# Output tiles split behind the row statistics, an MLP bank read earlier, the first tile's plane in halves, and attention's sums with ones at the head of a step

## The chip, the cores and the metric

One core of one Trainium2 chip. The time is device time in microseconds of one execution of the whole kernel. TensorE (PE) multiplies matrices into PSUM banks, VectorE (DVE), ScalarE (ACT) and GpSimd (POOL) do the elementwise work, and SyncE (SP) issues most DMAs. Each engine takes its instructions strictly in the order of its own queue.

## The reference

A bidirectional encoder block on a sequence of 1024 rows, width 1024, in float32:

```python
h = layer_norm(x, ln0_g, ln0_b)
proj = h @ w_in + b_in                 # 4352 columns: qa ka va qb kb vb ga gb
y_na  = neighbourhood_attention(qa, ka, va, na_rpb) @ w_branch_na
y_swa = windowed_gqa_with_sink(rope(qb), rope(kb), vb, sink) @ w_branch_swa
mixed = sigmoid(ga) * y_na + sigmoid(gb) * y_swa
h = layer_norm(ALPHA * h + mixed @ w_out + b_out, ln1_g, ln1_b)
u = square(relu(h @ w_ff1 + b_ff1))    # 4096 wide
h = layer_norm(ALPHA * h + u @ w_ff2 + b_ff2, ln2_g, ln2_b)
```

## The kernel before

**Numbers.** A float32 matrix is held as two float16 planes: the high plane is the matrix times a scale, rounded (made by ACT), the low plane is what the rounding left (made by DVE). A product is three PE matmuls for each slice of 128: high with high, high with low, low with high. The scale of a matrix comes from the sum of its squares: ACT squares with an accumulator, a small PE matmul with a matrix of ones adds up the partitions into two columns of a bank, DVE reads them, POOL raises them to a power. That matmul is the "sum with ones" (`total_of`, L194; its reader is `scale_of`, L200).

**Order.** The program runs under a manual schedule: each engine executes in the order in which the Python code issues instructions to it. So a moved line moves its instructions in each engine's queue. Stages that follow each other:

- *First layer norm* (8 tiles of 128 rows). Statistics on DVE, power on POOL, the norm itself on ACT (L369) or on DVE (L367) for the tiles listed in `NO_DVE` (index 2 and 3, which are tiles 6 and 7). PE turns each 128x128 block (L386), `ln0_turn` makes the planes `hT`, and gate projections run in between (L430).
- *Attention in 64 steps* (`steps`). A step issues scores for step s+2 (`part_a`: PE writes banks s and t, DVE reduces them, L783), then fill matmuls of the projections (`pump`), the exponentials and the low planes (`part_e`, `part_l`, whose planes are turned by DMA), more fill, the product with v (`part_c`), and the last fill. Jobs put off with `defer(n, ...)` become due after n fill matmuls and are issued by `flush`. Entry 2 of such a job says that it begins with PE work: sums with ones for the weights (L194), which write into spare columns of the newest score bank, and the turn of the softmax's reciprocals (L839). Both are issued by the `flush()` behind `part_c`.
- *Branch products* (`branch(f, half)`, 8 chunks of 128 columns by 2 halves). Bank gi=0 is the neighbourhood branch, gi=1 the window branch; DVE scales each bank with its gate (L1540), POOL adds the two into `mx` (L1542), ACT squares `mx` (`mx_square`, L1485). In the second half `between` issues the next chunk's sum with ones inside bank gi=1; in the very last one it issues `mx_scale(0)`: DVE adds the eight sums (`mx_sum`, L1489), PE totals (L1495), DVE reads (L1497), POOL takes the power (L1498), and `split_mx(0)` makes the planes of tile 0 (L1509 ACT, L1510 DVE).
- *Output products* for g = 0 to 7 (tiles of 128 rows), each in two banks of 512 columns (`out_mm`, L1637 to L1644). `out_evac` adds the residual and takes statistics (DVE, L1651 and L1655), `ln1_norm` finishes them (DVE L1659 and L1660, POOL L1661 and L283, ACT L285). The turn of tile g-1 (`turn`, L1672) stands in the middle of the second bank of tile g, its evacuation (`turn_evac`, ACT L1683 and DVE L1680) behind it, then `combine(g-1)` makes operand planes for the MLP (L1688, L1689; sums L1702 to L1706 from tile 4 on). `split_mx(g+2)` comes right behind the first bank's matmuls. `bound` (in g = 0) reads a bank of a small sum (DVE, L320) and computes a scale on POOL (L321 to L328), which `turn_evac(0)` uses. `late` (POOL, L1825) scales residual rows of later tiles. In g = 5 the first two weight slices of the MLP are split (`head_split`, L1736 ACT, L1739 DVE).
- *First MLP product* (16 column blocks p; `ff1_mm(p, i)`, L1812). Each block takes seven half-size products (a Strassen-Winograd scheme), i in the order 1, 2, 6, 5, 7, 3, 4, with weight sums (L1777) and operand sums S1 to S4. `after1(p, 1)` copies a bank (ACT, L1911) and settles the block before (ACT L1934, L1935 and a store), `after1(p, 2)` reads bank "s" (DVE, L1931). Bank "s" has two buffers. The first products run in the order (0,1) (0,2) (1,1) (1,2), turn of tile 7, (2,1) (2,2) (3,1) (3,2), (0,6) (1,6) (0,5) (1,5); `tick` prepares their weights, `comb_hi` and `comb_lo` their operands.
- *Second MLP product* (L2278) and the last layer norm.

Of the kernel before, what the change touches and what calls it, by code (L numbers as in the profile page):

```python
# [22 lines left out]
NCG = 8  # L23
# [46 lines left out]
STATS = {2: (4,), 3: (5,), 4: (6,)}  # L70
NO_DVE = 2, 3
NO0=4
# [21 lines left out]
def encoder_block(ctx, tc, x, w_in, w_br, w_out, w_ff1, w_ff2, par, rows, rpbp,  # L94
# [345 lines left out]

    def flush(pe=True, early=False, mid=False):
        for e in list(later):
            if e[0] <= 0 and (pe or not e[2]) and (e[3] or not early) and (early or not e[4] or not in_steps) \
                    and (mid or not e[5] or not in_steps):
                later.remove(e)
                e[1][0]()
                if e[1][1:]:
                    defer(*e[1][1:], early=e[3])
# [491 lines left out]
    with tc.manual_schedule(engines=MANUAL):  # L940
# [110 lines left out]
        def steps(s, n, before_b=None, before_c=None):  # L1051

            part = [int(n * SPLIT[0]), int(n * SPLIT[1])]
            part.append(n - sum(part))
            step_now[0] = s
            if s + 2 < 64:
                part_a(s + 2)
            pump(part[0])
            if before_b:
                before_b()  # L1060
            for op in bias_ops[:3]:
                bias_ops.pop(0)()
            flush(False, True)
            if 0 <= s + 1 < 64:
                part_l(s + 1)
            part_e(s + 2)
            if 0 <= s + 2 < 64 and (s + 2) % 8 == 7:
                norm_rows(heads[(s + 2) // 4].get()[5])
            flush(False, mid=True)
            pump(part[1])  # L1070
            if before_c:
                before_c()
            if s >= C_LAG:
                part_c(s - C_LAG)
            flush()
            pump(part[2])
# [399 lines left out]
        def tok(g):  # L1476
            return slice(g * P, (g + 1) * P)
# [14 lines left out]
        def mx_scale(half, ps, ones_, pw_):  # L1492
            if half == 0:
                mx_sum(0)
            PE.matmul(ps[:, 0:2], ones_, mtot[:, half:half + 1].to_broadcast([P, 2]), start=True, stop=True)  # L1495
# [7 lines left out]
        def split_mx(g):  # L1503

            if g < 2:
                xm.append(xps[g].tile([P, 2, 2, 8, P], F16, tag="m", name="m"))
            m = xm[g % 2][:, g // 2 % 2]
            mhl[g] = m[:, 0], m[:, 1]
            ACT.activation(m[:, 0], mx[:, :, tok(g)], AF.Copy, bias=0.0, scale=mx_sc(g, 0))  # L1509
            DVE.scalar_tensor_tensor(out=m[:, 1], in0=mx[:, :, tok(g)], scalar=mx_sc(g, 0), in1=m[:, 0],  # L1510
                                     op0=ALU.mult, op1=ALU.subtract)

# [14 lines left out]
        def branch(f, half, between=None):  # L1527
            both = []
            for gi, (act, tag) in enumerate(((o_na, "t"), (o_swa, "o"))):
                ps = psum(tag)  # L1530
                n = 2 if gi and between else 4
                gemm3(ps, bws[f], lambda part, k: act(part, k, half), nk=n, k0=4 * gi, last=(n == 4))
                if n == 2:
                    between()
                    gemm3(ps, bws[f], lambda part, k: act(part, k + 2, half), nk=2, k0=6, first=False)
                if (f, half, gi) == (7, 1, 1):
# [292 lines left out]
    with tc.manual_schedule(engines=MANUAL):  # L1829
# [10 lines left out]
        for g in range(NCG):  # L1840
            out_mm(g, 0, 0, 8)
            if g + 2 < NCG:
                split_mx(g + 2)
            if g + 2 < NCG:
                pre(g + 2)
# [25 lines left out]
            if 2 <= g < 6:  # L1871
                squares1(g - 2, raws[g - 2])
            if g == 5:
                head_split(0, 1)
                head_split(0, 2)
            out_evac(g, 1)
            ps = bound_sum() if g == 0 else None
            ln1_norm(g)
            if g == 0:
# [88 lines left out]
        ff1_mm(1, 2)  # L1968
        turn(7)
        turn_evac(7)  # L1970
        more_ring(1)
# [71 lines left out]
        tick()  # L2043
        after1(1, 1)
        after1(1, 2)
        tick()
# [525 lines left out]
```

## Time and profile before

| | |
|---|---|
| median of 3 runs | 1237.51 us (1237.05 to 1238.98) |
| the profiled execution's own time | 1237.68 us |
| its span, first to last instruction | 1235.7 us |
| granted PE clock | 0.998 |
| busy PE / DVE / ACT / POOL | 1210.1 / 976.1 / 867.3 / 333.9 us |
| attention's steps | about 85 to 388 us |
| branch products end, output products start | 548.8 us |
| output products end, first MLP product starts | 640.7 us |

A row of the timeline gives start, length (both us), engine, line, operation, output and inputs, shape and count; in brackets stands how long the engine had been idle and what ended that. Successive rows of an engine overlap by about 0.1 us, as an instruction's last part overlaps the start of the next. A row of the table of waits gives who waited for whom, the total, the number of times and the longest.

### The profile page before, as it was taken

How to read it: one execution, taken by the hardware profiler on the slowest of the kernel's cores; microseconds unless marked ns; L12 is line 12 of the kernel's file. 1: busy time of each engine (PE TensorE's matmuls, PEld its weight loads, DVE VectorE, ACT ScalarE, POOL GpSimd, SP SyncE). 2: the span in 40 equal slices, each digit the busy share in tenths (PEclk: the TensorE clock that was granted, in tenths of full speed). 3: DMA queues.
4: the chain of work that ended last, by engine and by line, in shares of the span. 5: the costliest groups of instructions: out<-in, count | busy, mean ns of one | idle time of the engine just before them, and what ended most of it. 6: DMA issues, size and time to landing. Idle time of an engine off the chain costs nothing.

```text
span 1235.7 us, 17241 instructions
## 1 busy us (share of the span) xinstructions
PE 1210.1 (98%) x6070; PEld 606.1 (49%) x6070; DVE 976.1 (79%) x1421; ACT 867.3 (70%) x1418; POOL 333.9 (27%) x368
## 2 busy tenths in 40 slices
PE   7999999999999999999999999999999999999997
PEld 5545555555555444444544444444444444444443
DVE  7687998878887975655798887887867778897888
ACT  7569889998886569743758878778775846344457
POOL 5212222433520013437620031333200002211207
PEclk9999999999999999999999999999999999999999
DMA  8654758777675346526513466776536536363333
GB/s 314 202 186 107 161 147 173 178 164 168 144 161 159 109 154 230 188 78 245 193 63 119 166 212 218 265 242 235 197 136 235 223 132 231 124 261 128 124 111 136
DMA packets 177878, 216.84 MB, mean 175 GB/s; under 512 B 111744, under 2 KB 125312, under 8 KB 171136
## 3 DMA queue, kind: packets, MB, share of 16 engines
q1 hardware_dynamic: 176816, 214.89, 54.7%
q8 instruction: 47, 0.77, 0.3%
q10 hardware_dynamic: 976, 0.87, 0.2%
q14 instruction: 39, 0.32, 0.1%
HBM read 130.69 MB, written 59.33 MB: 154 GB/s over the span
## 4 chain that ended last, share of the span: by engine, by line
PE 78%; DVE 8%; ACT 6%; issue 2%; POOL 2%; DMA 1%; SPq 0%; POOLq 0%; ACTq 0%; DVEq 0%
PE ps_mm L430 14%; PE ps_t L1812 6%; PE ps_o L1812 6%; PE ps_mm L1812 6%; PE ps_mm L2278 6%; PE ps_s L2278 6%; PE ps_t L2278 5%; PE ps_o L2278 5%; PE ps_s L1812 3%; PE ps_o L889 2%; PE ps_o L1178 2%; PE ps_mm L1178 1%; PE ps_t L1178 1%; PE ps_t L420 1%; PE ps_t L421 1%
## 5 line engine op out<-in xcount | busy, mean ns | idle before, releaser
L430 PE MATMUL ps_mm<-hT 128*128 128x512 f16 x960 | 226.4, 380 | 4.5 <-DVE hT L399 2.0
L1812 PEld LDWEIGHTS <-tw 128*128 128x128 f16 x1248 | 122.1, 99 | 145.0 <-DVE tw L1739 0.8
L2278 PEld LDWEIGHTS <-r1w 128*128 128x128 f16 x1008 | 98.7, 98 | 118.4
L430 PEld LDWEIGHTS <-hT 128*128 128x128 f16 x960 | 90.7, 99 | 102.0 <-issue 12.0
L802 ACT ACTIVATE ss<-ss,sk 128x384 f32<-128x384 f32 (+1 forms) x128 | 73.8, 578 | 25.3 <-DVE sk L783 25.1
L430 PE MATMUL ps_mm<-hT,wpair 128*128 128x512 f16 x288 | 68.8, 380 | 0.0
L1733 POOL TENSOR_TENSOR c<-c 128x2 f32<-128x2 f32 x16 | 15.6, 977 | 189.0 <-DVE c L1732 189.0
L2298 POOL TENSOR_TENSOR acc<-acc,rst 128x512 f32<-128x512 f32 x16 | 32.2, 2013 | 122.1 <-DMA rst<-xr_d 77.8
L201 POOL TENSOR_TENSOR hT<-hT 128x2 f32<-128x2 f32 x30 | 25.6, 852 | 114.1 <-DVE hT L200 114.1
L2112 ACT ACTIVATE hA<-r1w,c 128x2048 f16<-128x2048 f32 x10 | 20.0, 1996 | 50.0 <-DVE r1w L2167 26.8
L1739 DVE SCALAR_TENSOR_TENSOR tw<-raw,c,tw 128x512 f16<-128x512 f32 x60 | 51.2, 853 | 4.2 <-ACT tw L1736 3.9
L2115 DVE SCALAR_TENSOR_TENSOR r1w<-stg,c,r1w 128x2048 f16<-128x2048 f32 x21 | 49.6, 2360 | 4.0 <-ACT r1w L2112 4.0
L2278 PEld LDWEIGHTS <-hS 128*128 128x128 f16 x336 | 32.9, 98 | 39.4
L1178 PEld LDWEIGHTS <-hT 128*128 128x128 f16 x336 | 32.8, 99 | 38.6 <-DVE hT L1167 0.8
L889 PE MATMUL ps_o<-pt,vv 128*128 128x256 f16 (+1 forms) x448 | 49.2, 250 | 2.2 <-DMA pt<-hT 1.5
L814 DVE SCALAR_TENSOR_TENSOR pl<-ss,pl 128x768 f16<-128x768 f32 (+1 forms) x42 | 46.3, 1101 | 2.2 <-ACT pl L805 2.0
L1998 DVE TENSOR_TENSOR hS<-hS,hS 128x512 f32<-128x512 f32 x41 | 33.6, 820 | 14.6 <-ACT hS L1929 14.5
L889 PEld LDWEIGHTS <-vv 128*128 128x128 f16 x448 | 35.5, 98 | 19.3 <-DVE oT L898 1.9
L1812 PE MATMUL ps_t<-hS,tw 128*128 128x512 f16 x192 | 44.1, 379 | 0.3 <-DVE tw L1739 0.3
L1812 PE MATMUL ps_t<-r1w,tw 128*128 128x512 f16 x192 | 44.0, 379 | 0.0
L1812 PE MATMUL ps_o<-r1w,tw 128*128 128x512 f16 x192 | 44.0, 379 | 0.0
L1736 ACT ACTIVATE tw<-raw,c 128x512 f16<-128x512 f32 x60 | 41.8, 709 | 2.8 <-DVE raw L1777 2.8
(443 smaller groups left out, 3140.8 us busy)
## 6 DMA issues: line engine op xcount, KB each, us to landing
us_d<-hS SPq DMA_DIRECT2D x112, 256.0 KB, 3.1
stg<-us_d SPq DMA_DIRECT2D x28, 1024.0 KB, 4.8
raw<-in_w_ff SPq DMA_DIRECT2D x24, 512.0 KB, 5.6
r1w<-in_w_ff SPq DMA_DIRECT2D x10, 1024.0 KB, 7.6
sg<-sg_d SPq DMA_DIRECT2D x32, 256.0 KB, 2.9
hT<-in_w_in SPq DMA_DIRECT2D x60, 128.0 KB, 2.6
hA<-in_w_ff SPq DMA_DIRECT2D x6, 1024.0 KB, 8.2
hT<-in_w_in SPq DMA_DIRECT2D x11, 512.0 KB, 4.7
```

The lines of the kernel that those rows point to most:

```text
L430: PE.matmul(ps, a[:, k, :], act(b, k), start=(k == 0 and i == 0), stop=(k == NK - 1 and i == 2))
L802: ACT.activation(p, p, AF.Exp, bias=nm[:, i:i + 1], scale=-1.0, accum_out=sums_l[o_chunk][:, hh, 2 * t + i:2 * t + i + 1])
L814: DVE.scalar_tensor_tensor(out=pl[:, n:2 * n], in0=e[:, 0:n], scalar=P_SCALE, in1=pl[:, 0:n], op0=ALU.mult, op1=ALU.subtract)
L889: PE.matmul(o, vs, move(part), start=(m == 0 and part == 0), stop=(m == len(runs) - 1 and part == 1))
L1178: PE.matmul(ps, w[:, a, k, :], act[:, b, k, :], start=(first and k == 0 and m == 0), stop=(k == 3 and m == 2), skip_group_check=True)
L1736: ACT.activation(hi_lo(slot, 0), src, AF.Copy, bias=0.0, scale=w_scale(p))
L1739: DVE.scalar_tensor_tensor(out=hi_lo(slot, 1), in0=src, scalar=w_scale(p), in1=hi_lo(slot, 0), op0=ALU.mult, op1=ALU.subtract)
L1812: PE.matmul(ps, ww, act[:, part, k, :], start=(first and k == 0 and m == 0), stop=(k == 3 and m == 2), skip_group_check=True)
L1998: DVE.tensor_tensor(out=out, in0=a, in1=b, op=op)
L2115: DVE.scalar_tensor_tensor(out=slot[:, :, 1, :], in0=src, scalar=scale, in1=slot[:, :, 0, :], op0=ALU.mult, op1=ALU.subtract)
L2278: PE.matmul(ps, st[:, a, part, j * P:(j + 1) * P], w[:, a, wpart, :], start=(first and a == 0 and m == 0), stop=(a == 3 and m == 2), skip_ ...
L2298: POOL.tensor_tensor(out=z, in0=z, in1=t, op=ALU.add)
```

## The change

- The norms of tiles 6 and 7 of the first layer norm go to ACT (`NO_DVE` is empty).
- `flush` gets a `head` form, which issues only the jobs that begin with PE work; `steps` calls it first of all. The `flush` behind `part_c` no longer issues such jobs.
- In the branch products `between` is issued after one slice (three matmuls) of bank gi=1 and no longer after two. `mx_sum(0)` is issued ahead of the matmuls of bank gi=0 of the last chunk.
- `split_mx(0)` works in two halves of four slices each, on ACT and DVE in turn.
- In the output products `split_mx(g+2)` is issued behind `ln1_norm(g)`, and the two `head_split` of g = 5 as well. `bound` keeps its place in the text, and so comes behind the split of tile 2.
- `after1(1, 1)` and `after1(1, 2)` are issued right behind `turn(7)`, ahead of its evacuation.

```diff
--- before.py
+++ after.py
@@ -68,7 +68,7 @@
 PREP = 5, 6, 7, 8, 8, 9, 10, 12, 13, 14, 15, 16
 HI_ACT = (0, 2, 3, 4, 5), ()
 STATS = {2: (4,), 3: (5,), 4: (6,)}
-NO_DVE = 2, 3
+NO_DVE = ()
 NO0=4
 N_GATES = (2,), (3,), (4,), (), (5, 6, 7)
 SPLIT = .25, .45
@@ -438,9 +438,9 @@
 
         later.append([fns[0], fns[1:], pe, early or only, only, mid])
 
-    def flush(pe=True, early=False, mid=False):
+    def flush(pe=True, early=False, mid=False, head=False):
         for e in list(later):
-            if e[0] <= 0 and (pe or not e[2]) and (e[3] or not early) and (early or not e[4] or not in_steps) \
+            if e[0] <= 0 and (e[2] or not head) and (pe or not e[2]) and (e[3] or not early) and (early or not e[4] or not in_steps) \
                     and (mid or not e[5] or not in_steps):
                 later.remove(e)
                 e[1][0]()
@@ -1053,6 +1053,7 @@
             part = [int(n * SPLIT[0]), int(n * SPLIT[1])]
             part.append(n - sum(part))
             step_now[0] = s
+            flush(head=True)
             if s + 2 < 64:
                 part_a(s + 2)
             pump(part[0])
@@ -1072,7 +1073,7 @@
                 before_c()
             if s >= C_LAG:
                 part_c(s - C_LAG)
-            flush()
+            flush(False)
             pump(part[2])
 
         for n in range(0, N_PRE, 4):
@@ -1490,8 +1491,6 @@
                               op=ALU.add)
 
         def mx_scale(half, ps, ones_, pw_):
-            if half == 0:
-                mx_sum(0)
             PE.matmul(ps[:, 0:2], ones_, mtot[:, half:half + 1].to_broadcast([P, 2]), start=True, stop=True)
             t = mxc[:, 4:6]
             DVE.tensor_scalar(out=t, in0=ps[:, 0:2], scalar1=Q_MIN, scalar2=W_TOP ** -2, op0=ALU.max, op1=ALU.mult)
@@ -1506,9 +1505,10 @@
                 xm.append(xps[g].tile([P, 2, 2, 8, P], F16, tag="m", name="m"))
             m = xm[g % 2][:, g // 2 % 2]
             mhl[g] = m[:, 0], m[:, 1]
-            ACT.activation(m[:, 0], mx[:, :, tok(g)], AF.Copy, bias=0.0, scale=mx_sc(g, 0))
-            DVE.scalar_tensor_tensor(out=m[:, 1], in0=mx[:, :, tok(g)], scalar=mx_sc(g, 0), in1=m[:, 0],
-                                     op0=ALU.mult, op1=ALU.subtract)
+            for ks in (slice(0, 4), slice(4, 8)) if g == 0 else (slice(0, 8),):
+                ACT.activation(m[:, 0, ks], mx[:, ks, tok(g)], AF.Copy, bias=0.0, scale=mx_sc(g, 0))
+                DVE.scalar_tensor_tensor(out=m[:, 1, ks], in0=mx[:, ks, tok(g)], scalar=mx_sc(g, 0), in1=m[:, 0, ks],
+                                         op0=ALU.mult, op1=ALU.subtract)
 
         sg, sgs = {}, [(f, gi, half) for f in range(8) for half in range(2) for gi in range(2)]
 
@@ -1528,11 +1528,13 @@
             both = []
             for gi, (act, tag) in enumerate(((o_na, "t"), (o_swa, "o"))):
                 ps = psum(tag)
-                n = 2 if gi and between else 4
+                n = 1 if gi and between else 4
+                if (f, half, gi) == (7, 1, 0):
+                    mx_sum(0)
                 gemm3(ps, bws[f], lambda part, k: act(part, k, half), nk=n, k0=4 * gi, last=(n == 4))
-                if n == 2:
+                if n == 1:
                     between()
-                    gemm3(ps, bws[f], lambda part, k: act(part, k + 2, half), nk=2, k0=6, first=False)
+                    gemm3(ps, bws[f], lambda part, k: act(part, k + 1, half), nk=3, k0=5, first=False)
                 if (f, half, gi) == (7, 1, 1):
                     split_mx(0)
                 s_ = sg[f, gi, half]
@@ -1840,8 +1842,6 @@
         for g in range(NCG):
             out_mm(g, 0, 0, 8)
             if g + 2 < NCG:
-                split_mx(g + 2)
-            if g + 2 < NCG:
                 pre(g + 2)
             out_evac(g, 0)
             if g == 1:
@@ -1870,12 +1870,14 @@
                     head_hi(3, i, tsp.tile([P, 2, 512], F16, tag="ts", name="tws", bufs=4))
             if 2 <= g < 6:
                 squares1(g - 2, raws[g - 2])
+            out_evac(g, 1)
+            ps = bound_sum() if g == 0 else None
+            ln1_norm(g)
             if g == 5:
                 head_split(0, 1)
                 head_split(0, 2)
-            out_evac(g, 1)
-            ps = bound_sum() if g == 0 else None
-            ln1_norm(g)
+            if g + 2 < NCG:
+                split_mx(g + 2)
             if g == 0:
                 bound(ps)
             if g == 7:
@@ -1967,6 +1969,8 @@
         after1(0, 2)
         ff1_mm(1, 2)
         turn(7)
+        after1(1, 1)
+        after1(1, 2)
         turn_evac(7)
         more_ring(1)
         combine(7)
@@ -2041,8 +2045,6 @@
         load1(4)
         load1(5)
         tick()
-        after1(1, 1)
-        after1(1, 2)
         tick()
         ff1_mm(2, 2)
         comb_hi("S3")
```

## The prediction

> **What bounds the kernel now.** I read the page first, then the table of waits for TensorE (PE), then the timeline of each engine at the places that the change touches.
>
> ```profile
> span 1235.7 us, 17241 instructions
> ...
> PE 1210.1 (98%) x6070; PEld 606.1 (49%) x6070; DVE 976.1 (79%) x1421; ACT 867.3 (70%) x1418; POOL 333.9 (27%) x368
> ```
>
> PE is busy in 98% of the span, so 25.6 us are all that any reordering can win, and an edit is worth exactly the PE wait that it ends. A wait that it opens costs its whole length, because nothing later gives PE time back. The table of waits (what PE waited for: us in total, times, longest) holds what the edits aim at:
>
> ```profile
> PE ps_s L194 <- DVE sk L783: 1.9, 3, 0.8
> PE ps_t L1672 <- ACT z L285: 1.6, 1, 1.6
> ...
> PE ps_s L1812 <- DVE hS L1931: 1.3, 1, 1.3
> PE ps_t L386 <- ACT ln L369: 1.0, 1, 1.0
> PE ps_o L386 <- DVE ln L367: 0.9, 1, 0.9
> PE ps_mm L1637 <- ACT m L1509: 0.9, 1, 0.9
> ```
>
> L194 is a sum with ones in attention, L1672 the turn of an output tile, L1812 the first MLP product, L386 the turn at the start (the second of its rows is the norm on DVE that moves), L1637 the first output product. Together 6.6 us: that is the ceiling of the whole change. What it can lose has to be read from the engines behind PE.
>
> **Norms 6 and 7 of the first layer norm go from DVE to ACT.** The 0.9 us wait for L367 should shrink, as DVE has copies queued in front of the norm and ACT is freer there. But the next reader of that bank is ACT, which now holds two more passes, so the stretch behind it gains little. Between 0 and -0.9 I take **-0.3**, since ACT both gains and pays. A loss is not excluded, but needs ACT to be late for a whole plane; no row shows that.
>
> **Attention's sums go to the head of a step.** One of the three:
>
> ```profile
> 102.41 0.35 PE L194 MATMUL ps_s<-hT 128*128 128x2 f32 x2 [0.76 <-DVE sk L783]
> 102.62 1.02 PE L430 MATMUL ps_mm<-hT,wpair 128*128 128x512 f16 x4
> ```
>
> The sum writes into the bank of the newest scores, and DVE still reads them. In the new place four fill matmuls (about 0.9 us, second row) run before it, so the 0.76 us are covered; without that cover the sum costs what it costs now. The scores of the next step are issued behind the sum, 0.2 to 0.3 us later in such a step. The turns of the reciprocals move along, and with them ACT's copy, its store on ACT's own queue, and SP's load ten fill matmuls further on; neither has anything urgent behind it. Late next: DVE, which was the engine waited for. Where DVE sets the pace of later steps, part comes back. From -1.9 to +0.3 I take **-1.3**.
>
> **The sum over the mixed planes one bank earlier, its total three matmuls earlier, the first tile's plane in halves.** PE waits 0.9 us for the high plane of tile 0:
>
> ```profile
> 547.63 2.19 ACT L1509 ACTIVATE m<-mx,mxc 128x1024 f16<-128x1024 f32 x2 [2.12 <-POOL mxc L1498]
> ```
>
> One plane takes 1.1 us, half of it 0.55. Three matmuls are 0.65 us, of which the read by DVE gains about half, because the scaling of bank (7,1,0) is just in front of it. 0.55 + 0.3 = **-0.85**; bounds -0.5 (the half alone) and -0.9. For the other f the weight totals only come earlier, and their squares lie whole matmul groups before: nothing.
>
> **Splits behind the row statistics.** This is the large part, and I find that it loses. In the order of every queue a split now stands between a tile's row statistics and the combine of the tile before; it used to stand behind that combine. In tiles 1 to 4 the same work fills the same gap. Three things are not the same.
>
> First, tile 0. Its read of the bound's sum (DVE, L320) falls behind the split of tile 2. DVE rows, then POOL rows:
>
> ```profile
> 561.23 0.15 DVE L320 TENSOR_SCALAR c<-ps_o 128x2 f32<-128x2 f32 x1
> 564.66 1.28 DVE L1510 SCALAR_TENSOR_TENSOR m<-mx,mxc,m 128x1024 f16<-128x1024 f32 x1 [3.29 <-ACT m L1509]
> ...
> 562.27 0.71 POOL L321 TENSOR_TENSOR c<-c 128x2 f32<-128x2 f32 x1
> ...
> 566.13 5.17 POOL L1825 TENSOR_TENSOR zl<-zl 128x512 f32<-128x512 f32 x4
> 571.26 0.72 POOL L1498 TENSOR_TENSOR mxc<-mxc,c 128x2 f32<-128x2 f32 x1
> 572.90 0.55 POOL L1661 TENSOR_TENSOR mv<-mv,mhalf 128x1 f32<-128x1 f32 x1 [0.92 <-DVE mv L1660]
> ...
> 573.77 12.12 POOL L1825 TENSOR_TENSOR zl<-zl 128x512 f32<-128x512 f32 x8
> ```
>
> The read moves from 561.2 to about 565.9, the bound's seven POOL instructions start at 566.0 instead of 562.3: 3.8 us later. POOL then has no gap but the 0.9 us before L1661, so tile 1's power comes 2.9 us later, the 12.12 us of residual rows behind it too, and behind these tile 2's power: its norm is 2.9 us late.
>
> Second, the loop of tiles 2 to 5 (DVE, POOL, ACT) carries a delay on, since it is no faster than PE:
>
> ```profile
> 610.63 1.24 ACT L285 ACTIVATE zl<-zl,mv 128x1024 f32<-128x1024 f32 x1 [4.63 <-POOL mv L283]
> ...
> 624.28 1.24 ACT L285 ACTIVATE z<-z,mv 128x1024 f32<-128x1024 f32 x1 [4.73 <-POOL mv L283]
> ...
> 634.02 1.24 ACT L285 ACTIVATE z<-z,mv 128x1024 f32<-128x1024 f32 x1 [4.86 <-POOL mv L283]
> ...
> 612.54 1.04 PE L1672 MATMUL ps_t<-ident,zl 128*128 128x128 f32 x8
> ...
> 637.22 1.04 PE L1672 MATMUL ps_t<-ident,z 128*128 128x128 f32 x8
> ...
> 619.56 1.41 DVE L1739 SCALAR_TENSOR_TENSOR tw<-hA,c,tw 128x512 f16<-128x512 f32 x2
> ...
> 622.70 0.68 DVE L1702 TENSOR_TENSOR s1t<-mx 128x512 f32<-128x512 f32 x1
> ...
> 626.06 0.69 DVE L1689 TENSOR_TENSOR hS<-s2t,hS 128x512 f16<-128x512 f32 x1 [1.22 <-ACT hS L1688]
> ```
>
> (ACT's norms of tiles 4, 5 and 6; PE's turns of tiles 4 and 6; DVE's two low heads, the start of the combine of tile 4, its first low plane.) Tile 4's norm ends at 611.87 and its turn starts at 612.54: 0.7 us to spare, so 2.9 late makes PE 2.2 late. For tile 5 the heads (1.3 us net) leave the way: its norm starts at 624.28 + 2.9 - 1.3 = 625.9 and ends at 627.1. Its turn used to wait until 625.5 (the 1.6 us of the table); PE is then 1.6 us behind the old trace, and the old wait is not won.
>
> Third, tile 6. The old step from norm 5 to norm 6 is 634.02 - 624.28 = 9.74 us, and DVE used the latency of norm 5 for the combine of tile 4 (from 622.70, 1.6 us before norm 5 starts). Now in front of it stand: norm 5 on ACT (1.24), two high heads (taken as the 1.4 of the two low ones), the split's high half (1.1) and its low half (1.28), each needing the one before: 5.0 us after norm 5 starts. The combine is 6.6 us later; half of the 1.22 us wait inside it goes. 9.74 + 6.6 - 0.65 = 15.7, and 15.4 as rows overlap by some 0.1. Norm 6 runs from 641.3 to 642.5; its turn would come at 637.22 + 1.6 = 638.8. PE waits 3.7 us and is 5.3 us behind.
>
> **Bank of the second MLP product read before tile 7's planes.**
>
> ```profile
> 653.94 0.75 DVE L1931 SCALAR_TENSOR_TENSOR hS<-ps_s,c,sn 128x512 f32<-128x512 f32 x1
> 654.74 2.75 PE L1812 MATMUL ps_s<-hA,twx 128*128 128x512 f16 x12
> ...
> 672.65 0.61 PE L1812 MATMUL ps_t<-hS,tw 128*128 128x512 f16 x2 [0.31 <-DVE tw L1739]
> ```
>
> Product (2,2), second row, starts as DVE has just read the bank of (0,2), first row. DVE is now as late as norm 6, 641.3 - 634.0 = 7.3 us, and PE only 5.3, so PE waits 2.0 more. At (3,2) the 1.3 us of the table go, as intended. But the settling that moves along puts two ACT passes, which wait for that late DVE row, ahead of tile 7's planes; the planes feed S2, and the combined planes feed (0,6) to (1,5). At (1,5), last row, PE was already waiting (0.31) for a low plane, so it takes over their delay: 7.3 us, and up to 1.2 more for the two passes. The 1.3 is given back there. For splits and bank together I take **+7.5**; bounds +8.5 and +3, the low end being a loop in which DVE is never held up by POOL (below).
>
> **Sum.** -0.3 - 1.3 - 0.85 + 7.5 = +5.05. The profiled execution took 1237.68 us with its 1235.7 us span; the median of the three runs is 1237.51 (1237.05 to 1238.98), so nothing shifts between them. 1237.5 + 5.0 = **1242.5 us**.
>
> **Rivals.** (a) *Row statistics really come first, and the kernel gets faster.* For no wait at turn 6, norm 6 must end at 637.22 - 1.6 = 635.6, so norm 5 must start by 635.6 - 1.24 - 15.4 = 619.0, 5.3 us ahead of the old 624.28; from there the edit wins. For it: PE leaves DVE room, as tile 5's products end well before its evacuation. Against it: the heads give only 1.3, and the bound takes 2.9. Then 1.6 + 1.3 + 2.45 are won: 1232.2 us.
>
> (b) *The loop gets shorter, and little is left.* The low split takes 1.28 us where POOL runs small instructions, but:
>
> ```profile
> 578.54 2.29 DVE L1510 SCALAR_TENSOR_TENSOR m<-mx,mxc,m 128x1024 f16<-128x1024 f32 x1
> ```
>
> Here POOL runs its residual rows (12.12 us from 573.77). If the moved splits miss those rows, three loops win 1.0 us each: norm 5 starts at 622.9, its turn does not wait (PE -0.3), norm 6 ends at 639.5 against 636.9 (PE +2.3), and the late DVE makes it about +4.5 by (1,5): 1237.5 - 2.45 + 4.5 = 1239.5 us. Against it: POOL starts those rows right behind each norm's scalars, just where the split goes now. [...]
>
> (c) *Attention and the first tile win nothing.* DVE is the engine waited for in attention, and the reduction may only be waited for one step later: 1237.5 + 7.5 = 1245 us.
>
> **How the numbers follow.** Forecast 0.50, (a) 0.14, (b) 0.20, (c) 0.16. The likeliest alone reaches from 1240 to 1246 (the stage's +3.5 to +8.5 with the small gains). The range of 8 in 10, 1234.5 to 1246.5, takes in (b), (c) and the near part of (a). About 0.2% (2.5 us) is what the spread of the runs lets a measurement tell from no change. Forecast and (c) are slower: 0.66; (b) is the same, 0.20; (a) is faster, 0.14.
>
> **What would show it.** Right: no PE wait at L194 and L1637; L320 at about 566, POOL's bound behind it, a PE wait at the turn of tile 2; DVE idle between tile 5's statistics and its first head; the longest PE wait of the middle, 3 to 4 us, at the turn of tile 6; no wait of (3,2), but 2 us at (2,2). Wrong: norm 5 before 620, or a turn of tile 6 that follows its products at once; then the time is below 1236.

## The result, and the profile after

| | before | after |
|---|---|---|
| median of the runs, us | 1237.56 | 1248.04 (1247.65 to 1249.21) |
| ratio, 95% interval | | 1.0084 [1.0067, 1.0102] |
| the profiled execution's own time, us | 1237.68 | 1247.65 |
| its span, us | 1235.7 | 1245.5 |

The changed kernel is slower by about 10.5 us; 5 us were forecast. Of all executions behind the numbers below one stands apart, an execution of 3298 us of the first experiment's kernel: its median of 1244.16 counts it (1244.06 without it), its ratio does not.

Most lines of `after` stand one or two higher than those of before: the turn of an output tile is L1674 (was L1672), the first MLP product L1814 (L1812), the read of a bank L1933 (L1931), the first output product L1639 (L1637). First the page's busy times and the table of waits of the kernel after (us in total, times, longest):

```profile
PE 1215.5 (98%) x6070; PEld 607.8 (49%) x6070; DVE 967.3 (78%) x1420; ACT 869.8 (70%) x1421; POOL 329.1 (26%) x368
...
PE ps_t L1674 <- ACT z L285: 4.7, 2, 4.0
PE ps_s L194 <- DVE sk L783: 3.4, 3, 1.8
PE ps_o L889 <- DMA pt<-hT: 2.1, 1, 2.1
...
PE ps_t L1814 <- DVE tw L1741: 0.9, 1, 0.9
PE ps_mm L1814 <- DVE twx L1741: 0.9, 1, 0.9
...
PE ps_s L1814 <- DVE hS L1933: 0.4, 1, 0.4
```

Of the rows shown of before, those of L1637 and of the norm on DVE (L367) are gone. L194 has not gone: it grew from 1.9 to 3.4. L1672's 1.6 became 4.7, and the sixth and fifth products (L1814; banks mm and t) have new waits.

PE issues the same matmuls in both kernels up to the few that move, so the shift of one and the same matmul tells where time went. Rows of PE's timeline, before first:

```profile
30.68 1.46 PE L430 MATMUL ps_mm<-hT 128*128 128x512 f16 x6
387.12 0.82 PE L889 MATMUL ps_o<-pt,vv 128*128 128x256 f16 x8
548.83 3.41 PE L1637 MATMUL ps_mm<-r1w,m 128*128 128x512 f16 x15 [0.90 <-ACT m L1509]
```

and after:

```profile
29.85 1.46 PE L430 MATMUL ps_mm<-hT 128*128 128x512 f16 x6
389.88 0.82 PE L889 MATMUL ps_o<-pt,vv 128*128 128x256 f16 x8
550.78 3.41 PE L1639 MATMUL ps_mm<-r1w,m 128*128 128x512 f16 x15
603.87 1.09 PE L1674 MATMUL ps_t<-ident,zl 128*128 128x128 f32 x8 [0.50 <-ACT zl L285]
643.75 1.97 PE L1674 MATMUL ps_t<-ident,z 128*128 128x128 f32 x8 [4.03 <-ACT z L285]
663.17 2.75 PE L1814 MATMUL ps_s<-hA,twx 128*128 128x512 f16 x12 [0.38 <-DVE hS L1933]
668.35 2.75 PE L1814 MATMUL ps_s<-hA,tws 128*128 128x512 f16 x12
682.48 2.33 PE L1814 MATMUL ps_t<-hS,tw 128*128 128x512 f16 x10 [0.93 <-DVE tw L1741]
```

With the rows that the prediction shows of before for products (2,2), (3,2) and (1,5), the shifts are:

| place | shift, us | since the place above | forecast |
|---|---|---|---|
| first layer norm (30.68 to 29.85; -0.55 by 73 us) | -0.83 | -0.55 kept | -0.3 |
| end of attention's steps (387.12 to 389.88) | +2.76 | **+3.3** | **-1.3** |
| first output product (548.83 to 550.78) | +1.95 | -0.8 | -0.85 |
| (2,2) (654.74 to 663.17) | +8.43 | +6.5 | |
| (3,2) (661.39 to 668.35) | +6.96 | -1.5 | |
| (1,5) (672.65 to 682.48) | +9.83 | +2.9, in all +7.9 | +7.5 |
| whole execution (1237.68 to 1247.65) | +9.97 | | +5 |

Part by part the forecast is within half a us, but for attention, where a gain of 1.3 us was a loss of about 3.3. Of that part the single execution is a rough measure: in four kernels below that have the same program up to there, the first output product starts at 551.01 to 552.99 us, not at 550.78.

Attention's rows show the mechanism. SP's load of the reciprocals and DVE's scaling that reads them, before:

```profile
133.41 1.17 SPq L852 DMA_DIRECT2D rb<-rl_d  x2
141.07 0.75 DVE L860 SCALAR_TENSOR_TENSOR oT<-oT,vs,rb 128x512 f32<-128x512 f32 x1
```

and after, with the score reduction behind it on DVE and the sum with ones on PE:

```profile
136.17 1.18 SPq L852 DMA_DIRECT2D rb<-rl_d  x2
140.97 0.75 DVE L860 SCALAR_TENSOR_TENSOR oT<-oT,vs,rb 128x512 f32<-128x512 f32 x1 [1.32 <-DMA rb<-rl_d]
141.63 0.61 DVE L783 CUSTOM_DVE_ANT_0 ss<-ps_s,bd,snk 128x384 f32<-128x384 f32 x1
142.40 0.35 PE L194 MATMUL ps_s<-hT 128*128 128x2 f32 x2 [1.00 <-DVE sk L783]
175.75 0.35 PE L194 MATMUL ps_s<-hT 128*128 128x2 f32 x2 [1.76 <-DVE sk L783]
```

The turn of the reciprocals itself is not late (125.67 us against 126.20). But SP's load is a job that becomes due ten fill matmuls after the turn, and it is issued by a `flush`. A step here has four fill matmuls behind the product with v and eight ahead of it. From the old place of the turn (behind the product with v) twelve pass before the next `flush` behind that product; from the new one (the head of the step) only eight, so the load is not yet due there and goes with a later `flush`: behind another transposing DMA, 2.8 us later in time while the work around it is about 1.4 us earlier. So DVE, which takes its queue in order, idles 1.32 us ahead of the scaling, the score reduction behind that is late, and the sum, which now stands at the head of the step, waits for that reduction instead of running behind it. DVE idles for this DMA three times, 4.3 us in all, and in the kernel before not once; the longest wait of the sum is the one at 175.75 us.

### The profile page after: what moved, and what is told of

Read it like the earlier page. It is cut to its first block, busy times and chain, and to the rows that moved or that the text cites. A ratio compares the mean times of both kernels' runs of the same rounds, so it can differ in the third digit from the quotient of the medians.

```text
span 1245.5 us, 17241 instructions
## 1 busy us (share of the span) xinstructions
PE 1215.5 (98%) x6070; PEld 607.8 (49%) x6070; DVE 967.3 (78%) x1420; ACT 869.8 (70%) x1421; POOL 329.1 (26%) x368
## 5 line engine op out<-in xcount | busy, mean ns | idle before, releaser
L1814 PEld LDWEIGHTS <-tw 128*128 128x128 f16 x1248 | 121.9, 99 | 146.2 <-DVE tw L1741 1.8
L889 PE MATMUL ps_o<-pt,vv 128*128 128x256 f16 (+1 forms) x448 | 49.5, 251 | 2.1 <-DMA pt<-hT 2.1
L1814 PE MATMUL ps_t<-hS,tw 128*128 128x512 f16 x192 | 44.2, 379 | 1.2 <-DVE tw L1741 0.9
L889 PEld LDWEIGHTS <-vv 128*128 128x128 f16 x448 | 35.6, 98 | 19.5 <-issue 2.4
L1814 PE MATMUL ps_t<-r1w,tw 128*128 128x512 f16 x192 | 44.0, 379 | 0.0
L1814 PE MATMUL ps_o<-r1w,tw 128*128 128x512 f16 x192 | 44.0, 379 | 0.0
```

Source lines behind the costliest of these rows:

```text
L889: PE.matmul(o, vs, move(part), start=(m == 0 and part == 0), stop=(m == len(runs) - 1 and part == 1))
L1814: PE.matmul(ps, ww, act[:, part, k, :], start=(first and k == 0 and m == 0), stop=(k == 3 and m == 2), skip_group_check=True)
```

## The experiments

Times are medians in us, and "over before" is against the kernel before, timed beside it on the same chip. In code, `...` stands for lines not shown. The changed kernel is +10.5 over before.

**Attention back as it was.**

```diff
-            flush(head=True)
-            flush(False)          # behind part_c
+            flush()
```

> The changed kernel with attention's jobs that begin with PE work issued behind part_c again, as before the change; all else as changed. Against the kernel before, the changed kernel's matmuls are 0.55 us early at the start of attention's steps and 2.8 us late at their end, so the theory that the loss sits in these steps expects 3 to 3.5 us back: about 1244.6 us, PE's waits of attention as before (1.9 us at L194 in three, 1.5 at L889), and no half-clock stretch near 214 us. The rival, that the extra time is the lower granted clock of the whole run, expects at most 1.7 us back. Both leave the output products as they are (7.9 us lost between 548 and 672 us of the old trace).

1244.16, +6.9 over before, ratio 1.0053 [1.0040, 1.0066]. So the attention edit costs 3.6 us (10.5 - 6.9), and the rest of the change is about what the forecast says of it (-0.3 - 0.85 + 7.5 = +6.35).

**Only the turn of the reciprocals back behind the product with v**, the sums with ones staying at the head.

```diff
...
-        defer(10, turn, pe=True)
+        defer(10, turn, pe='tail')    # issued by the flush behind part_c
...
```

> As changed, but only the turn of the softmax's reciprocals (L839) goes back behind part_c; the sums with ones stay at the head of a step. Theory R: the sums are not what costs; the turn at the head lets SP issue the load of the reciprocals 2.8 to 4.3 us later, DVE waits for it in front of the scores (1.3, 2.1 and 0.9 us at L860), and PE's sum behind those scores. Then the waits at L860 and L194 go, attention wins about 1.5 us against the kernel before, and the whole takes 1242.5 to 1243.5 us. Rival P: the place at the head is itself the cost, as the scores come behind the sum; then L194 still waits about 3 us and the time stays near 1247.5 us.

1243.21, +5.9 over before, ratio 1.0050 [1.0038, 1.0062]. No wait at L194 is left. The moved turn is the part that loses (10.5 - 5.9 = 4.6 us), and the sums with ones at the head gain about 1 (6.9 to 5.9; the two intervals overlap). Here the first output product starts at 546.46 us, 2.4 us ahead of the kernel before.

**Only SP's load back in its place**, everything else as in the changed kernel; only SP's queue differs.

```diff
-                defer(10, lambda: load_recip(o_chunk))
+                defer(4, lambda: load_recip(o_chunk))
```

> The changed kernel with one number changed: SP's load of the softmax's reciprocals becomes due 4 fill matmuls behind their turn instead of 10, which puts it back to its old place in SP's queue, one step earlier. Every other queue is the same. Theory (the late load alone makes DVE's scaling wait, and with it the next score reduction and the sum at the head): the scaling at L860 does not wait for that DMA, the waits at L194 are gone, and the time falls by 4 to 5 us as with the whole turn put back: 1243 to 1244. Rival (the turn at the head costs by itself, on PE, ACT or in the bank): 1247 to 1248.

1243.77, +6.65 over before, ratio 1.0054 [1.0041, 1.0068]. Rows of SP and DVE of this kernel:

```profile
131.76 1.16 SPq L852 DMA_DIRECT2D rb<-rl_d  x2
139.42 0.75 DVE L860 SCALAR_TENSOR_TENSOR oT<-oT,vs,rb 128x512 f32<-128x512 f32 x1
```

The scaling no longer waits, L194 is gone from the table of waits, the first output product starts at 546.94 us instead of 550.78, and 10.5 - 6.65 = 3.85 us are back. The due time of one DMA was most of what the moved turn costs.

**The splits of the output tiles back**, with the two `head_split`; the bank read early stays.

```diff
             if g + 2 < NCG:
+                split_mx(g + 2)         # behind the first bank's matmuls
...
+            if g == 5:
+                head_split(0, 1)
+                head_split(0, 2)
             out_evac(g, 1)
             ps = bound_sum() if g == 0 else None
             ln1_norm(g)
-            if g == 5:
-                head_split(0, 1)
-                head_split(0, 2)
-            if g + 2 < NCG:
-                split_mx(g + 2)
```

> As changed, but the splits of the output products and the two head splits of tile 5 stand where they stood before (behind the first bank, ahead of the second evacuation); the earlier bank reads of the MLP stay. Theory: the moved splits cost the 4.0 us at the turn of tile 6 and 0.5 at that of tile 2, and through DVE's lateness the waits at the start of the MLP; with them back, the old wait of 1.6 us at tile 5 returns, the turn of tile 6 does not wait, and 4.5 to 6.5 us come back: 1241 to 1243 us. Rival: the earlier bank reads are the larger part of the loss; then less than 3 us come back and waits at (0,6) and (1,5) stay.

1242.79, +5.5 over before, ratio 1.0045 [1.0033, 1.0057]: the moved splits cost 5.0 us (5.8 by the shifts from the first output product to (1,5), +2.1 here against +7.9). What is left of that stage's loss, 2.1, falls to the bank, the only other edit there.

**`bound` ahead of the split of tile 2.**

```diff
             ln1_norm(g)
+            if g == 0:
+                bound(ps)
             if g == 5:
...
             if g + 2 < NCG:
                 split_mx(g + 2)
-            if g == 0:
-                bound(ps)
```

> As changed, but in tile 0 the bound is read ahead of the split of tile 2 (one call moved). The prediction had this read push POOL back by 2.9 us and all norms after it. If so, L320 is back at about 561 us in old time, POOL's residual rows start 2.9 us sooner, the wait at the turn of tile 2 goes (0.5 us), and the one at tile 6 falls by up to 2.9 us, from 4.0 to between 1 and 2: 1244 to 1246 us. Rival: DVE's own queue sets the loop, not POOL; then the turn of tile 6 still waits over 3 us and the time stays within 1 us of 1247.6.

1246.30, +9.0 over before, ratio 1.0075 [1.0063, 1.0087], just above what the theory expected (1244 to 1246) and just below what its rival did (within 1 us of 1247.6). DVE's read and the table of waits of this kernel:

```profile
564.46 0.15 DVE L320 TENSOR_SCALAR c<-ps_o 128x2 f32<-128x2 f32 x1
...
PE ps_t L1674 <- ACT z L285: 4.0, 1, 4.0
```

The read of the bound's sum comes 12.4 us behind the first output product (552.06 here), as in the kernel before, where the changed kernel has 17.0 (567.82). The waits at the turns of tiles 3 and 5 (0.5 and 0.7) are gone. But the 4.0 us at tile 6 stay, as the rival said: PE comes to that turn earlier by as much as norm 6 does. The bound's place is worth 1.5 us, 1.9 by the shifts (+6.0 instead of +7.9 in the stage).

**The step of tile 5 put in order**: heads and the split of tile 7 behind the combine of tile 4.

```diff
-            if g == 5:                  # behind ln1_norm
-                head_split(0, 1)
-                head_split(0, 2)
-            if g + 2 < NCG:
+            if g + 2 < NCG and g != 5:
                 split_mx(g + 2)
...
                 combine(g - 1)
+            if g == 5:
+                head_split(0, 1)
+                head_split(0, 2)
+                split_mx(7)
```

> The changed kernel with only the step of tile 5 reordered: the two head splits and the split of tile 7 stand behind combine(4), so that nothing stands between tile 5's row statistics and that combine; the splits of tiles 2 to 6 stay behind the statistics. Theory (the chain norm 5, high heads, split, combine, norm 6 makes the 4.0 us wait at the turn of tile 6 and the late DVE): that wait falls to 0 to 0.8 us, product (2,2) does not wait, and the time falls by 3 to 4.5 us: 1243.5 to 1245. Rival (DVE is late by the sum of its work, and the order within one tile only shifts the wait): the wait at tile 6 falls but comes back at (2,2), (0,6) or (1,5); 1247 to 1248.

1245.67, +8.1 over before, ratio 1.0062 [1.0050, 1.0075]. Rows of PE:

```profile
634.12 0.39 PE L1646 MATMUL ps_mm<-r1w,m 128*128 128x512 f16 x1 [1.14 <-DVE m L1510]
641.47 1.04 PE L1674 MATMUL ps_t<-ident,z 128*128 128x128 f32 x8
660.24 2.75 PE L1814 MATMUL ps_s<-hA,twx 128*128 128x512 f16 x12 [1.32 <-DVE hS L1934]
```

The turn of tile 6 (641.47) follows its products with no wait: the chain named in the prediction made those 4 us. Of them 2.4 are kept over the whole kernel; 1.1 come back as a wait for tile 7's plane, and (2,2) waits 1.3 instead of 0.4. That lies between the two theories, nearer the first.

**The bank alone**, on the kernel before.

```diff
         turn(7)
+        after1(1, 1)
+        after1(1, 2)
         turn_evac(7)
...
         tick()
-        after1(1, 1)
-        after1(1, 2)
         tick()
```

> The kernel before with only the edit of the bank of the second MLP product: it is read ahead of tile 7's planes. By the prediction's reading (1.3 us won at the third block's second product, given back at the fifth products since two ACT passes stand ahead of tile 7's planes): 1237.3 to 1238.3, no measurable change, with the wait at product (3,2) gone and one of about 1 us at (0,6), (0,5) or (1,5) instead. If the gain stays: 1236.0 to 1236.5. If the edit costs the 2.1 us that it cost with the changed attention and norms in front of it: 1239.3.

1238.70, +1.4 over before, ratio 1.0012 [1.0003, 1.0021]: more than the prediction's reading gave (1238.3 at most), less than the 2.1 us that the edit seemed to cost in the changed kernel. Rows of ACT, then of PE:

```profile
654.50 0.63 ACT L1934 ACTIVATE hS<-hS 128x512 f32<-128x512 f32 x1 [2.17 <-DVE hS L1931]
...
659.69 2.75 PE L1812 MATMUL ps_s<-hA,tws 128*128 128x512 f16 x12
...
673.81 1.47 PE L1812 MATMUL ps_t<-hS,tw 128*128 128x512 f16 x6 [0.93 <-DVE tw L1739]
```

(3,2) comes 1.7 us earlier than before (661.39), as meant, and (1,5) 1.2 us later (672.65). ACT settles block 0 ahead of tile 7's evacuation and sits idle 2.17 us for DVE's row; the planes behind it, and what the fifth products need, are late by that. More than given back.

**The parts that gained**: splits, bank and the turn of the reciprocals where they were; norms 6 and 7 on ACT, the sums at the head and the first tile's edits kept. (The diff is the sum of the ones above.)

> The changed kernel without the three parts that were found to cost: the splits of output tiles stand where they were, the bank is read where it was, and the turn of the softmax's reciprocals comes behind the product with v again. What stays: norms 6 and 7 on ACT, the sums with ones at the head of a step, the first tile's plane in halves with its total earlier. The prediction's own gains for these, -0.3, -1.3 and -0.85, give 1235.0. If attention's gain is taken back by waits for the planes turned by DMA: 1236.2. If parts that cost cannot be told apart like this (their waits come back elsewhere): 1237.3 or more.

1235.38, 1.9 us under before, ratio 0.9985 [0.9976, 0.9994]: the three parts were forecast to give 2.45.

**The same with the bank read early and settled late.**

```diff
         turn(7)
+        snap(1, "s1", banks[1, "a"])
+        act_fn(1, 1, "A11", banks[1, "b"], snaps[1, "s1"], 0)
         turn_evac(7)
...
-        after1(1, 1)
-        after1(1, 2)
+        waiting.pop(0)()                # settles block 0 only
```

> On the kernel of parts that gained (1235.4 us): the bank of product (1,2) is read ahead of tile 7's evacuation, as in the change, but of what moved along only the two reads of banks (one ACT copy, one DVE pass) stay there; the settling of block 0's two ACT passes is left at its old place. Theory (the ACT passes, which wait for a late DVE row, are what the bank edit costs): the wait at product (3,2) is gone, tile 7's evacuation is only 0.7 us later instead of 2.4 to 3, and by the fifth products the time is within 0.5 us of the kernel it builds on: 1234.9 to 1235.9. If the gain at (3,2) stays: 1234.2. Rival (any bank read ahead of tile 7's planes costs, whatever settles): 1236.3 to 1237.

1235.15, 2.4 us under before, ratio 0.9976 [0.9967, 0.9985], the best median of all kernels here (the interval overlaps that of the kernel it builds on), and 2.4 + 10.5 = 12.9 under the changed one. Against the kernel that it builds on, (3,2) comes 1.9 us earlier and (1,5) 0.4: the two ACT passes that settle block 0 were the cost, and most of the gain at (3,2) is given back at the fifth products.

**The heads behind the combine**, also on the parts that gained.

```diff
-            if g == 5:                  # ahead of out_evac(g, 1)
-                head_split(0, 1)
-                head_split(0, 2)
...
                 combine(g - 1)
+            if g == 5:
+                head_split(0, 1)
+                head_split(0, 2)
```

> On the kernel of parts that gained (1235.4 us): only the two head splits of tile 5 move, from ahead of its second statistics to behind combine(4). Theory (row statistics first is right where what is put back is not needed soon, and is put behind the combine and not ahead of it): norm 5 starts 1.3 us earlier, the 1.6 us wait at the turn of tile 5 falls to 0.3, norm 6 is no later, and the time is 1234.0 to 1234.5. Rival (DVE's work is only moved, and ends as late at the fifth products): the wait is gone at tile 5 and comes back later; 1235.2 to 1235.8.

1235.78, ratio 0.9985 [0.9976, 0.9994], the same as without the edit (1235.38). Rows of PE:

```profile
622.96 1.09 PE L1674 MATMUL ps_t<-ident,z 128*128 128x128 f32 x8 [0.73 <-ACT z L285]
653.52 2.75 PE L1814 MATMUL ps_s<-hA,twx 128*128 128x512 f16 x12 [1.46 <-DVE hS L1933]
660.18 2.75 PE L1814 MATMUL ps_s<-hA,tws 128*128 128x512 f16 x12 [1.32 <-DVE hS L1933]
```

The rival held: the wait at the turn of tile 5 fell from 1.64 to 0.73, and (2,2) and (3,2) wait 2.8 in place of 0.6. DVE does the same work, and PE meets it later.

**The moved turn with its load in time**, on the best kernel: `defer(10, turn, pe=True)` and `defer(4, ...)` for the load.

> The kernel of parts that gained with the bank read early and settled late (1235.15 us), with the turns of the reciprocals at the head of a step as in the change and their load due 4 fill matmuls behind them instead of 10. If the moved turn is worth nothing by itself: 1235.15 within 0.5 us. If it ends a wait: 1234.0 to 1234.6. If it costs by itself: 1236 to 1239.

1236.10, 1.0 us under before, ratio 0.9990 [0.9981, 0.9998], against 2.4 under before without it (the two intervals just overlap): in the range expected if the moved turn costs by itself. The row of its table of waits:

```profile
PE ps_t L839 <- DVE hT L200: 1.5, 1, 1.5
```

At the head the turn comes so soon behind DVE's reciprocal that PE waits for it. (The row names L200, which ended last; but in the changed kernel the turn at 225.30 us started ahead of that L200, at 225.48, so the turn does not need it.) The turn had better stay where it was.

**PE kept busy ahead of a wait.** Two kernels add matmuls whose results are thrown away, one in attention and one ahead of the turn of tile 6, to see what the half clock does that the changed kernel shows there (last section).

```diff
...
+            for _ in range(18):         # ahead of part_c of step 28; po is that product's own bank
+                PE.matmul(po[:, 256:512], hT[:, 0, 0, 0:P], hT[:, 0, 0, 0:256], start=True, stop=True)
```

> The changed kernel with 18 extra matmuls of 256 columns (about 0.11 us each, 2.0 us together) issued in step 28 just ahead of the product with v that waited 2.1 us for a DMA at 213 us; their results are thrown away by the product's own first matmul. So PE has the same stretch without useful work, but is not idle in it. Clock theory (the half clock of 3.4 us behind that wait comes from PE's idleness): no half clock near 214 us, and some 1 to 1.7 us less than the changed kernel: 1246.3 to 1247. Rival (the granted clock has its own times, whatever PE does, or the wait only hides a time that comes back later): the same time as the changed kernel, 1248.0 within 0.5, or up to 1 us more from the extra matmuls.

1248.72, ratio 1.0090 [1.0076, 1.0104]: no gain. In PE's rows (the changed kernel's first) the half clock's 1.7 us are won by 216 us, although this execution came into the step 0.9 us later, and lost ten us on, where the turn of the reciprocals waits for DVE (as it does, 1.45 us, in the next kernel, which has the full clock there without a fill):

```profile
216.87 1.90 PE L430 MATMUL ps_mm<-hT 128*128 128x512 f16 x8
...
216.02 1.90 PE L430 MATMUL ps_mm<-hT 128*128 128x512 f16 x8
226.06 0.28 PE L839 MATMUL ps_t<-ident,rl 128*16 128x128 f32 x1 [1.48 <-DVE hT L200]
```

```diff
+            if g == 7:                  # ahead of turn(6)
+                fp = psum("o")
+                for x in range(18):
+                    PE.matmul(fp, mhl[7][0][:, x % 8, :], wo[:, 0, x % 8, 0:512], start=True, stop=True)
```

> The changed kernel with 18 extra matmuls of 512 columns (about 3.9 us together) issued in tile 7's output product just ahead of the turn of tile 6, where PE waits 4.0 us for its norm. Clock theory: no half clock of 3.4 or 6.8 us near 640 to 650 us. If PE is what sets the end behind it, 1.7 to 3.4 us less: 1244.6 to 1246.3. Rival (DVE and ACT, late by norm 6, set the end at the fifth products anyway, as the sum said): no half clock, but product (2,2) then waits 1.5 to 2 us for DVE instead of 0.4, and the time stays at 1247.5 to 1248.5.

1248.74, ratio 1.0092 [1.0078, 1.0106]: no gain, 0.2 above the rival's range. PE's row of (2,2):

```profile
665.31 2.75 PE L1814 MATMUL ps_s<-hA,twx 128*128 128x512 f16 x12 [1.92 <-DVE hS L1937]
```

Without the half clock PE meets DVE 1.9 us early, and from the first output product to (1,5) the stage loses 7.8 us, as in the changed kernel (7.9). In both places PE's speed was not what set the end.

## Why the prediction was right or wrong

**Attention's sums: wrong, and this carries nearly the whole miss.** The step that failed is the sentence that the turns of the reciprocals, ACT's copy, the store and SP's load move along and "neither has anything urgent behind it". It counted how late the load would be in fill matmuls ("ten fill matmuls further on") and not at which place of the step a job that is due gets issued, nor who reads the load: DVE's scaling, ahead of the next score reduction in DVE's queue. The range went down to a gain of 1.9 and allowed a loss of 0.3; measured was a loss of 3.3 by the shifts and 3.6 by putting the edit back, and 3.85 us went when SP's due time alone was changed. The cover for the sums, the rest of that part, was read rightly: with the turn put back, or the load in time, no PE wait at L194 is left, and the sums win about 1 us (1.3 forecast). With the turn put back the time is 1243.21, 0.7 from the forecast.

**Tile 6: right in mechanism, and the sum of the stage right partly by luck.** ACT's norms of tiles 5 and 6 and DVE's work between them:

```profile
626.61 1.24 ACT L285 ACTIVATE z<-z,mv 128x1024 f32<-128x1024 f32 x1 [4.82 <-POOL mv L283]
...
642.46 1.24 ACT L285 ACTIVATE z<-z,mv 128x1024 f32<-128x1024 f32 x1 [4.85 <-POOL mv L283]
...
628.56 1.42 DVE L1741 SCALAR_TENSOR_TENSOR tw<-hA,c,tw 128x512 f16<-128x512 f32 x2 [3.04 <-ACT tw L1738]
630.15 1.28 DVE L1510 SCALAR_TENSOR_TENSOR m<-mx,mxc,m 128x1024 f16<-128x1024 f32 x1 [0.18 <-ACT m L1509]
631.36 0.68 DVE L1704 TENSOR_TENSOR s1t<-mx 128x512 f32<-128x512 f32 x1
```

DVE idles 3.04 us ahead of the first low head, as was said. The combine starts 4.75 us after norm 5 (5.0 forecast), norm 6 15.85 us after norm 5 (15.4), the turn of tile 6 waits 4.0 us (3.7). Product (2,2) was to wait 2.0 us; it waits 0.4, because PE had lost 1.7 to the half clock by then, and 1.92 where that was kept away. By (1,5) the stage lost 7.9 (7.5 forecast). But in that forecast the late norm 6 made 7.3 and the bank almost nothing; with the splits put back the stage still loses 2.1, so the splits made 5.8 and the bank 2.1 (1.4 alone). One term too large and one too small cancelled.

**Tile 0 and the bound: right in place, smaller in effect.** L320 was forecast at 565.9 and came at 567.82, of which 1.95 is the shift brought along. PE was to be 2.2 us late by tile 4 and 1.6 at tile 5. Less the 1.95, the turn of tile 4 is late by 1.3 (612.54 to 615.79) and that of tile 5 by 0.4, and why it is less stays open; the wait shows at the turn of tile 3 (603.87, 0.5 us), not of tile 2. Putting the bound first gave back 1.5.

**First layer norm and first tile: right.** -0.55 (forecast -0.3) and -0.8 (-0.85); the waits at L367 and L1637 are gone.

**The bank: right that it is given back, too mild.** The wait at (3,2) went, as forecast. Alone the edit costs 1.4 us, and the two ACT passes named in the prediction are the cause: with them left behind it costs nothing.

**Rival (b) was set aside for a wrong reason.** Against it stood that POOL starts its residual rows just where the split goes now. It does, but the split does not take longer for it. The rows of DVE (before, then after) and of POOL (after):

```profile
588.58 3.00 DVE L1689 TENSOR_TENSOR hA<-mx,hA 128x512 f16<-128x512 f32 x2 [3.92 <-ACT hA L1688]
591.50 2.29 DVE L1510 SCALAR_TENSOR_TENSOR m<-mx,mxc,m 128x1024 f16<-128x1024 f32 x1
...
593.01 1.28 DVE L1510 SCALAR_TENSOR_TENSOR m<-mx,mxc,m 128x1024 f16<-128x1024 f32 x1 [4.50 <-ACT m L1509]
594.21 3.43 DVE L1691 TENSOR_TENSOR hA<-mx,hA 128x512 f16<-128x512 f32 x2
...
593.13 2.29 POOL L1827 TENSOR_TENSOR zl<-zl 128x512 f32<-128x512 f32 x1
```

The moved split takes 1.28 us although residual rows run (1.28 to 1.32 in all four tiles where it took 2.15 to 2.29 before): it starts 0.12 us ahead of one of POOL's pieces, and it is that piece which takes 2.29. The low planes behind it pay (3.43 for two, 3.00 before), and DVE's work is 0.6 us shorter in this tile. The gain bought nothing, as DVE sat idle for ACT ahead of it, 3.4 to 4.6 us in these tiles. In the four tiles the moved split starts 0.12 to 0.21 us ahead of a piece of POOL's, which takes 2.24 to 2.29 (the one before it 1.27 or 1.28); in the kernel before it started 0.39 to 0.53 us behind the start of a piece, which took 1.60. In all eight the one that started second is the longer one; no run changes that order alone. That the split would be held up in its new place too was the author's estimate; these rows show the opposite.

**Rivals (a) and (c).** For (a) norm 5 had to start by 619.0 in the time of the kernel before; it started at 626.61, or 624.66 less the 1.95. (c) had the sign of attention's part nearly right (nothing won), but named DVE's pace, where a late DMA took more than the sums gained.

**The range.** The likeliest case's "1240 to 1246" does not come out of its own bounds: these add up to 1236.8 to 1245.8, and the stage's low end is +3 in one place and +3.5 in another. The measured 1248.04 lies above all of them.

**"An edit is worth exactly the PE wait that it ends": too simple.** Taking 0.9 us off the 1.6 us wait at tile 5 was worth nothing, since DVE's queue was no shorter and PE waited for it 30 us on; the same holds for (3,2), and for the half clock's 1.7 us in both fills.

## What to carry to other kernels

When a job moves in a software schedule, follow everything that it makes due later to the place where it will then be issued, and from there to its reader: here one DMA, issued 2.8 us late, cost nearly 4 us, where the moved sums gained about 1. A wait of the busiest engine is worth its length only if the engine waited for gets shorter or has room later; where it stayed as long, the wait turned up again a few products on (of 1.9 us won at (3,2), 0.4 was left at (1,5)). Put back-filled work behind what the next stage needs (the combine), not only behind the statistics: in tile 5 that kept 2.4 us.

## What the runs showed of the hardware that was not expected

PE's busy time rose by 5.4 us for the same work. Two stretches in which PE was granted half its clock make about 3.4 us of that (half of twice 3.41); the rest is not explained here. Stretches of the timeline (start and end, length, busy times, then PEclk, the granted share of the clock, DMA share and GB/s): two of the changed kernel, then the kernel with the fill in attention.

```profile
213.43:216.84 3.41, 3.41 (x14) 2.29 (x12) 3.41 (x6) 3.34 (x7) 3.41 (x5) 0.50 0.71 186
643.51:646.92 3.41, 3.17 (x12) 2.28 (x13) 2.68 (x5) 3.41 (x8) 0.00 (x0) 0.50 0.37 154
...
214.00:217.41 3.41, 3.41 (x22) 2.21 (x21) 3.41 (x7) 3.04 (x7) 3.41 (x6) 1.00 0.81 209
```

The granted clock is half for 3.41 us, once behind the 2.13 us wait at L889 (which ended at 213.23 us) and once about the end of the 4.0 us wait at tile 6. With matmuls put into the first wait the clock stays full (last row). That alone does not show that the idle time was the cause, for the kernel with the fill at tile 6 has nothing put in there, waits as long at the same place, and has the full clock behind it:

```profile
215.45 0.71 PE L889 MATMUL ps_o<-pt,vv 128*128 128x256 f16 x6 [2.09 <-DMA pt<-hT]
...
215.45:218.86 3.41, 3.41 (x21) 2.22 (x21) 3.41 (x5) 3.34 (x7) 3.33 (x5) 1.00 0.93 240
```

So the length of such a wait does not decide alone. Behind the 1.64 us wait at the turn of tile 5 it is the same: the kernel of the parts that gained has a half-clock stretch (first row), and the kernel before, with a wait of the same length there, has none (second row).

```profile
624.44:627.85 3.41, 3.41 (x10) 1.19 (x9) 3.38 (x9) 2.00 (x6) 0.48 (x1) 0.50 0.15 56
...
625.57:631.00 5.43, 5.43 (x32) 3.19 (x33) 4.91 (x11) 3.59 (x9) 0.91 (x2) 1.00 0.26 101
```

At the turn of tile 6 six kernels here wait 3.7 to 4.0 us. In the changed kernel, one of them, the half clock lies about the end of that wait; the kernel with matmuls in that wait is granted the full clock there (1.00 from 640 to 648 us). What starts such a stretch, and what sets its length, is not shown by any run here.
